# The tokens' half-precision copies: contiguous reads and strided writes in place of strided reads and contiguous writes

## The chip, the cores and the metric

The kernel runs on one core of a Trainium2 chip. The metric is the device time of one execution in microseconds (us); lower is better. The time of a version is the median of its runs. A core has a matrix engine (PE, with its weight loads listed apart as PEld), a vector engine (DVE), an activation engine (ACT), a general engine (POOL), and a queue engine (SP) that here issues nearly all large transfers.

## What is computed

One layer of a streaming encoder over 512 tokens of width 1024. A token mixer (gated spatial mixing beside differential attention) is followed by a layer norm, and then by a mixture of experts: 32 experts in 4 groups, two experts for each token.

```python
def _hier_moe(x, w_group, b_group, w_expert, b_expert, w_gate, w_up, w_down):
    t = x.reshape(B * S, D)
    ...
    def expert_block(args):
        tok, wgt, e = args
        xb = t[tok]
        hb = jax.nn.silu(xb @ w_gate[e]) * (xb @ w_up[e])
        return (hb @ w_down[e]) * wgt[:, None].astype(xb.dtype)
```

In `reference` the result of the mixer goes through `h = _layer_norm(ALPHA * h + mix, ...)`, then `ffn = _hier_moe(h, ...)`, and `_layer_norm(ALPHA * h + ffn, ...)` is the output.

## The kernel before, in words

The first 470 us are the mixer and the router. After the first layer norm the tokens lie in four tiles `h[t]`, each 128 tokens by 1024 channels in single precision; the router has counted each token's place within its expert in `RS`.

The experts are worked through in 13 steps that the code calls pairs (`PER` lists how many experts share a step: 2 or 4). For each step p:

- `gate_up(p, xe)` (L1159, matmuls at L1170) multiplies the step's gathered tokens `xe` by the gate and up weights.
- `slot_info` (L1228) reads token number and weight of each place, `glu` (L1250) forms silu times up, `glu_transpose` (L1257) transposes it.
- `down` (L1277) multiplies by the down weights; `combine` (L1285) spreads the results back over the tokens, and they are added into `y[t]`, which is the same memory as `h[t]`.
- In between, `gather_mm` (L1220, matmuls at L1224) gathers the tokens of the next step with a one-hot matrix made by `one_hot` (L1212, DVE at L1216).

`gather_mm` needs half-precision weights. So each `h[t]`, scaled by 1024, is kept as the sum of two half-precision pieces, `hs[t][0]` and `hs[t][1]`. `split_h(t)` (L1198) makes them: ACT rounds `h[t]` to the first piece (L1202), DVE subtracts that from `h[t]` and rounds the rest to the second (L1203). These run once per kernel, for t = 0 to 3: four ACT and four DVE instructions, each over 128 partitions by 1024 elements.

The pieces are stored in another order than `h[t]`. Channel 4m + i of `h[t]` lies at place 256i + m of a piece, so that `part_block` (L1195) can hand a contiguous block of 128 to each weight load.

The order around the split is fixed by the code (`manual_schedule`, L1635 on): the first `one_hot`, then the four `split_h`, then the second `one_hot`, then step 0. The second `one_hot` stands behind the four DVE instructions of the split on DVE's queue, and the gather in step 0 needs both it and the pieces. On PE's queue the gather stands behind `gate_up(0)` and `slot_info(0)`. The pieces' tiles, `HS`, take memory that was used in the stage before, among it by the tile of weights `sF` that `gate_up(0)` reads.

Weights come in 1 MB chunks into a ring of buffers (`AHEAD` = 21 chunks ahead, L668). SP issues the load of a chunk when the matmuls that read the buffer's former chunk are done, so PE's progress sets when transfers start. After step 0's gather DVE's queue holds the sorting of the experts (L1373 to L1385), eight instructions of `scale_h` (L1209, L1210) and the second part of the first down result (L1282).

Of the kernel before, what the change touches and what calls it, by code (L numbers as in the profile page):

```python
# [48 lines left out]
def hybrid_block(ctx: ExitStack, tc: tile.TileContext, x, w_in, b_in, sg_ln_g, sg_ln_b, sg_w, sg_b,  # L49
# [35 lines left out]
    def mkpool(stack, name, side):  # L85
        return stack.enter_context(tc.tile_pool(name=name, bufs=1, side=side, reuse_waits="tile"))
# [553 lines left out]
    hp = mkpool(ctx, "hp", "left")  # L640
    h = [hp.tile([128, D], F32, name=f"h{t}") for t in range(NT)]
# [449 lines left out]
    with tc.manual_schedule():  # L1091
# [51 lines left out]
        t = NT - 1  # L1143
# [44 lines left out]
    hs = {}  # L1188
# [8 lines left out]

    def split_h(t):  # L1198
        hs[t] = [HS[t // 2][:, 2 * (t % 2) + j] for j in range(2)]
        hp = h[t].rearrange("q (m i) -> q i m", i=4)  # L1200
        ha, hb = [v.rearrange("q (i m) -> q i m", i=4) for v in hs[t]]
        S.activation(ha, hp, AF.Copy, scale=HSCALE)  # L1202
        V.scalar_tensor_tensor(hb, hp, HSCALE, ha, op0=OP.mult, op1=OP.subtract)  # L1203

# [430 lines left out]
    with tc.manual_schedule():  # L1635
        load_chunks(0, AHEAD + 7)
        ohf = one_hot(0)
        for t in range(NT):
            split_h(t)
        nxt = one_hot(1)  # L1640
        tok1 = mv.tile([128, T], F32, name="tok1", tag="tok1")
        G.iota(tok1, pattern=[[1, T]], base=1, channel_multiplier=0, allow_small_or_imprecise_dtypes=True)
        for p in range(OVERFLOW_AFTER + 1):
            gu, ohf, nxt, xe = pair(p, gu, ohf, nxt)
# [36 lines left out]
```

## Time and profile before

| what | value |
|---|---|
| median of 3 runs | 952.56 us |
| lowest and highest run | 948.33 and 954.31 us |
| the profiled execution's own time | 953.16 us |
| its span, from first to last instruction | 951.6 us |
| PE busy | 901.0 us (95%) |
| DVE busy | 428.1 us (45%) |
| ACT busy | 292.8 us (31%) |
| PE's mean granted clock, share of full speed | 0.982 |

The profiled execution takes 1.56 us more than its span, for what lies around it, and is 0.60 us above the median. Busy shares are means over stages with different limits, so a row is read in the stretch in which it stands. In the rows below, a line as L1202 is the line of the kernel, `out<-in` are the program's tiles, and `128x1024` is partitions by elements.

### The profile page before, as it was taken

How to read it: one execution, taken by the hardware profiler on the slowest of the kernel's cores; microseconds unless marked ns; L12 is line 12 of the kernel's file. 1: busy time of each engine (PE TensorE's matmuls, PEld its weight loads, DVE VectorE, ACT ScalarE, POOL GpSimd, SP SyncE). 2: the span in 40 equal slices, each digit the busy share in tenths (PEclk: the TensorE clock that was granted, in tenths of full speed). 3: DMA queues.
4: the chain of work that ended last, by engine and by line, in shares of the span. 5: the costliest groups of instructions: out<-in, count | busy, mean ns of one | idle time of the engine just before them, and what ended most of it. 6: DMA issues, size and time to landing. Idle time of an engine off the chain costs nothing.

```text
span 951.6 us, 13677 instructions
## 1 busy us (share of the span) xinstructions
PE 901.0 (95%) x5231; PEld 583.1 (61%) x5232; DVE 428.1 (45%) x904; ACT 292.8 (31%) x527; POOL 58.0 (6%) x114
## 2 busy tenths in 40 slices
PE   8999999999999999999989999776779999999997
PEld 6989898986888888888844444222224444444434
DVE  3557676767953333244776332203013342233236
ACT  3356475667841332232441110101001111011213
POOL 5010101011010100020000000000000000000002
PEclk9999999999999999999999999998889999999999
DMA  8535343533143377865587999999999999999972
GB/s 223 144 108 154 91 137 96 137 105 104 63 118 89 121 277 253 295 247 200 192 322 291 417 419 419 419 419 419 418 418 419 420 417 421 418 420 419 389 236 89
DMA packets 80598, 256.11 MB, mean 269 GB/s; under 512 B 9112, under 2 KB 30672, under 8 KB 59536
## 3 DMA queue, kind: packets, MB, share of 16 engines
q1 hardware_dynamic: 79216, 252.36, 70.4%
q0 software_dynamic: 1312, 2.83, 1.4%
q8 instruction: 43, 0.70, 0.3%
q14 instruction: 27, 0.22, 0.1%
HBM read 244.67 MB, written 2.10 MB: 259 GB/s over the span
## 4 chain that ended last, share of the span: by engine, by line
PE 75%; DMA 15%; DVE 7%; ACT 1%; issue 1%; SPq 0%; DVEq 0%; ACTq 0%
PE ps_acc L1170 14%; PE ps_acc L142 7%; PE ps_acc L143 7%; PE ps_acc L144 7%; PE ps_acc L1272 7%; PE ps_w L142 4%; PE ps_w L143 4%; PE ps_w L144 4%; PE ps_w L1289 4%; PE ps_acc L1224 3%; DMA sE<-in_w_down_dram 3%; DMA sO<-in_w_gate_dram 2%; DMA sZ<-in_w_up_dram 2%; DMA sW<-in_w_gate_dram 2%; DMA sS<-in_w_up_dram 2%; DMA sX<-in_w_down_dram 2%
## 5 line engine op out<-in xcount | busy, mean ns | idle before, releaser
L119 DVE TENSOR_TENSOR sW<-wraw,sW 128x1024 fp32r<-128x1024 f32 (+1 forms) x38 | 46.5, 1224 | 98.6 <-ACT sW L118 98.5
L118 ACT CAST sW<-wraw 128x1024 fp32r<-128x1024 f32 (+1 forms) x38 | 39.1, 1030 | 117.5 <-PE ps_w L144 65.8
L142 PE MATMUL ps_acc<-sX,sW 128*128 128x512 f32 x184 | 73.3, 398 | 0.0
L144 PE MATMUL ps_acc<-sX,sW 128*128 128x512 f32 x184 | 72.2, 393 | 0.0
L143 PE MATMUL ps_acc<-sX,sW 128*128 128x512 f32 x184 | 72.0, 391 | 0.0
L1239 DVE TENSOR_REDUCE tid<-ps_w 128x1 f32<-128x2 f32 x11 | 1.7, 159 | 144.4 <-PE ps_w L1234 144.4
L1170 PE MATMUL ps_acc<-sX,xe 128*64 128x512 f32 (+1 forms) x176 | 58.2, 616 | 7.2 <-DMA sX<-in_w_up_dram 7.2
L1282 DVE SCALAR_TENSOR_TENSOR olo<-ps_acc,ws,ohi 128x512 fp32r<-128x512 f32 x22 | 16.5, 750 | 107.8 <-ACT ohi L1281 107.8
L1170 PE MATMUL ps_acc<-sO,xe 128*64 128x512 f32 (+1 forms) x240 | 62.0, 603 | 2.9 <-DMA sO<-in_w_gate_dram 1.5
L1224 PEld LDWEIGHTS <-hs 128*128 128x128 f16 x768 | 45.5, 100 | 21.3 <-issue 21.1
L1292 DVE TENSOR_TENSOR h<-h,ps_w 128x512 f32<-128x512 f32 x88 | 54.4, 679 | 7.9 <-PE ps_w L1289 7.9
L1281 ACT ACTIVATE ohi<-ps_acc,ws 128x512 fp32r<-128x512 f32 x22 | 15.1, 687 | 133.2 <-PE ps_acc L1272 128.3
L1224 PE MATMUL ps_acc<-oh,hs 128*128 128x128 f16 x768 | 52.0, 223 | 2.8 <-DVE oh L1216 2.8
L1170 PE MATMUL ps_acc<-sE,xe 128*64 128x512 f32 (+1 forms) x168 | 50.7, 683 | 1.4 <-DMA sE<-in_w_gate_dram 1.4
L1170 PE MATMUL ps_acc<-sS,xe 128*64 128x512 f32 (+1 forms) x152 | 49.6, 594 | 1.4 <-DMA sS<-in_w_up_dram 1.4
L1170 PE MATMUL ps_acc<-sW,xe 128*64 128x512 f32 (+1 forms) x112 | 45.4, 622 | 5.8 <-DMA sZ<-in_w_up_dram 5.8
L1272 PE MATMUL ps_acc<-sS,hT 128*32 128x512 f32 (+1 forms) x112 | 42.6, 631 | 2.8 <-DMA sS<-in_w_down_dram 2.8
L1170 PE MATMUL ps_acc<-sZ,xe 128*64 128x512 f32 (+1 forms) x120 | 40.3, 609 | 1.5 <-DMA sZ<-in_w_up_dram 1.5
L262 DVE TENSOR_TENSOR sW<-wraw,sW 128x1024 fp32r<-128x1024 f32 x31 | 38.3, 1241 | 6.3 <-ACT sW L258 6.3
L1263 ACT COPY hT<-ps_w 128x512 f32<-128x512 f32 x11 | 6.4, 585 | 112.2 <-PE ps_w L1260 112.2
L1272 PE MATMUL ps_acc<-sW,hT 128*32 128x512 f32 (+1 forms) x80 | 35.1, 646 | 5.1 <-DMA sW<-in_w_down_dram 5.1
L144 PEld LDWEIGHTS ps_acc<-sX,sW 128*128 128x128 f32 x184 | 34.5, 188 | 7.4
(399 smaller groups left out, 2000.0 us busy)
## 6 DMA issues: line engine op xcount, KB each, us to landing
wraw<-in_w_in_dram SPq DMA_DIRECT2D x32, 512.0 KB, 3.7
sX<-in_w_up_dram SPq DMA_DIRECT2D x16, 1024.0 KB, 17.9
sS<-in_w_down_dram SPq DMA_DIRECT2D x14, 1024.0 KB, 17.5
sO<-in_w_up_dram SPq DMA_DIRECT2D x14, 1024.0 KB, 19.8
sO<-in_w_gate_dram SPq DMA_DIRECT2D x13, 1024.0 KB, 19.7
sX<-in_w_down_dram SPq DMA_DIRECT2D x13, 1024.0 KB, 16.0
sS<-in_w_gate_dram SPq DMA_DIRECT2D x12, 1024.0 KB, 16.1
sE<-in_w_gate_dram SPq DMA_DIRECT2D x12, 1024.0 KB, 19.8
```

The source lines that it names most:

```text
L118: S.copy(hi, src)
L119: V.tensor_sub(lo, src, hi.bitcast(F32))
L142: P.matmul(o, lhsT=lh, rhs=rh, start=first, stop=False)
L143: P.matmul(o, lhsT=lh, rhs=rl, start=False, stop=False)
L144: P.matmul(o, lhsT=ll, rhs=rh, start=False, stop=last)
L262: V.tensor_sub(usplit[i][1], uraw[i], usplit[i][0].bitcast(F32))
L1170: P.matmul(o[j * w:(j + 1) * w, :], lhsT=xe[:, k, j * w:(j + 1) * w], rhs=chunk(p, m, j, k), start=k == ks[0], stop=k == ks[-1], skip_grou ...
L1224: P.matmul(pg[d // 4][:, (d % 4) * 128:(d % 4 + 1) * 128], lhsT=part_block(hs[t][j], d), rhs=ohf[:, t], start=d % 4 == 0 and t == 0 and j ...
L1272: P.matmul(po[j * w:(j + 1) * w, :], lhsT=hT[:, k, j * w:(j + 1) * w], rhs=chunk(p, 2 + n, j, k), start=k == 0, stop=k == 3, skip_group_ch ...
L1282: V.scalar_tensor_tensor(ol, po, ws, oh.bitcast(F32), op0=OP.mult, op1=OP.subtract)
L1289: P.matmul(pcs[t], lhsT=ohT[:, t * 128:(t + 1) * 128], rhs=o, start=i == 0, stop=i == 1)
L1292: V.tensor_add(yn, yn, pcs[t])
```

## The change

`split_h` walks both operands in another order. Before, the inner loop of each instruction goes over m: the single-precision input is read with a step of 4 elements (16 bytes) and the half-precision output is written one element after the other. After the change the inner loop goes over i: the input is read in memory order, and each output element lands 256 elements (512 bytes) from the one before it. Every fourth element starts a new run, 2 bytes on. The DVE instruction has the first piece, `ha`, as its second input; it is read in the same order as the output is written, in memory order before and with the step of 512 bytes after.

```diff
     def split_h(t):
         hs[t] = [HS[t // 2][:, 2 * (t % 2) + j] for j in range(2)]
-        hp = h[t].rearrange("q (m i) -> q i m", i=4)
-        ha, hb = [v.rearrange("q (i m) -> q i m", i=4) for v in hs[t]]
+        hp = h[t].rearrange("q (m i) -> q m i", i=4)
+        ha, hb = [v.rearrange("q (i m) -> q m i", i=4) for v in hs[t]]
         S.activation(ha, hp, AF.Copy, scale=HSCALE)
         V.scalar_tensor_tensor(hb, hp, HSCALE, ha, op0=OP.mult, op1=OP.subtract)
```

The values and where they are stored stay the same. Nothing moves: every engine has the same instructions in the same order, and only the access patterns of the four ACT and four DVE instructions differ.

## Rows read from the trace of the kernel before

**Rows 1.** The page, part 1 (busy time and share of the span) and, from part 2, the DMA rate in 40 equal slices of 23.8 us each.

```profile
PE 901.0 (95%) x5231; PEld 583.1 (61%) x5232; DVE 428.1 (45%) x904; ACT 292.8 (31%) x527; POOL 58.0 (6%) x114
...
GB/s 223 144 108 154 91 137 96 137 105 104 63 118 89 121 277 253 295 247 200 192 322 291 417 419 419 419 419 419 418 418 419 420 417 421 418 420 419 389 236 89
```

**Rows 2.** The chain of waits from 440 to 560 us, in order of time: start, length, what.

```profile
471.38 2.75 PE ps_acc L1170 x12
474.14 5.56 DMA sE<-in_w_down_dram
479.70 7.95 DVE hs L1203 x4
487.65 0.61 DVE oh L1216
488.30 1.86 PE ps_acc L1224 x16
```

**Rows 3.** The timeline from 464 to 512 us: start, length, engine, line, operation; in brackets the idle time before it and what ended it.

```profile
474.87 0.20 ACT L1052 ACTIVATE warm<-eps_c 128x1 f32<-128x1 f32 x1
...
476.38 0.69 DVE L1216 TENSOR_TENSOR oh<-io,RW 128x512 f16<-128x512 f32 x1
...
476.51 1.03 PE L1170 MATMUL ps_acc<-sF,xe 128*64 128x512 f32 x4
...
477.58 8.07 ACT L1202 ACTIVATE hs<-h 128x1024 f16<-128x1024 f32 x4 [2.51 <-PE ps_acc L1170]
...
479.69 7.96 DVE L1203 SCALAR_TENSOR_TENSOR hs<-h,hs 128x1024 f16<-128x1024 f32 x4 [2.62 <-DMA sE<-in_w_down_dram]
...
485.38 0.10 PEld L1224 LDWEIGHTS <-hs 128*128 128x128 f16 x1
...
487.56 0.68 DVE L1216 TENSOR_TENSOR oh<-io,RW 128x512 f16<-128x512 f32 x1
...
488.30 1.86 PE L1224 MATMUL ps_acc<-oh,hs 128*128 128x128 f16 x16 [2.75 <-DVE oh L1216]
...
489.96 1.06 PE L1260 MATMUL ps_w<-ident,sl 128*128 128x128 f32 x4
```

**Rows 4.** The two lines of the split, instruction by instruction: shortest, median and longest in ns, first and last start in us.

```profile
L1202 ACT ACTIVATE hs<-h x4: 2075/2093/2115, 477.6 to 483.6; 128x1024 f16<-128x1024 f32 x4
```

```profile
L1203 DVE SCALAR_TENSOR_TENSOR hs<-h,hs x4: 1958/2047/2072, 479.7 to 485.7; 128x1024 f16<-128x1024 f32 x4
```

**Rows 5.** Groups by line with shapes kept apart, over the whole span: busy us and mean ns of one, then idle time before. All but the two last read and write in memory order; those two are the split's.

```profile
L118 ACT CAST sW<-wraw 128x1024 fp32r<-128x1024 f32 x36 | 37.9, 1053 | 116.0 <-PE ps_w L144 65.8 <-PE ps_acc L144 29.1 <-DMA wraw<-in_w_out_dram 11.7
```

```profile
L501 DVE SCALAR_TENSOR_TENSOR hsel<-hw 128x1024 fp32r<-128x1024 f32 x1 | 1.2, 1192 | 0.0
```

```profile
L1202 ACT ACTIVATE hs<-h 128x1024 f16<-128x1024 f32 x4 | 8.1, 2094 | 2.5 <-PE ps_acc L1170 2.5
```

```profile
L1203 DVE SCALAR_TENSOR_TENSOR hs<-h,hs 128x1024 f16<-128x1024 f32 x4 | 8.0, 2031 | 2.6 <-DMA sE<-in_w_down_dram 2.6
```

**Rows 6.** The same groups in the stretch from 470 to 510 us, for one line at two sizes. L1070 writes half-precision elements 6 bytes apart (every third place of a tile).

```profile
L1070 DVE TENSOR_SCALAR W<-RW 128x104 f16<-128x104 f32 x1 | 0.3, 260 | 0.0
...
L1070 DVE TENSOR_SCALAR W<-RW 128x24 f16<-128x24 f32 x1 | 0.2, 186 | 0.0
```

**Rows 7.** Busy time by stretches of 2.5 us: PE, PEld, DVE, ACT and POOL (with counts), then PE's granted clock, the DMA share and GB/s.

```profile
485.00:487.50 2.50, 0.55 (x10) 0.29 (x9) 2.50 (x2) 1.13 (x2) 0.00 (x0) 1.00 0.99 419
487.50:490.00 2.50, 1.70 (x17) 1.70 (x17) 2.12 (x7) 0.00 (x0) 0.00 (x0) 0.61 1.00 423
490.00:492.50 2.50, 2.50 (x27) 2.08 (x26) 0.95 (x9) 1.07 (x2) 0.00 (x0) 0.70 1.02 429
492.50:495.00 2.50, 2.50 (x17) 0.97 (x16) 1.96 (x6) 0.10 (x1) 0.00 (x0) 1.00 0.55 229
```

**Rows 8.** The timeline of PE alone from 515 to 527 us: the same matmuls in the next step of the experts.

```profile
522.55 1.05 PE L1224 MATMUL ps_acc<-oh,hs 128*128 128x128 f16 x16
523.90 0.75 PE L1260 MATMUL ps_w<-ident,sl 128*128 128x128 f32 x4 [0.29 <-DVE sl L1253]
```

**Rows 9.** Busy time by longer stretches, columns as in rows 7.

```profile
495.00:500.00 5.00, 4.44 (x39) 2.73 (x35) 4.86 (x11) 0.69 (x1) 0.00 (x0) 1.00 0.77 257
500.00:505.00 5.00, 4.36 (x19) 1.92 (x21) 3.93 (x11) 0.00 (x0) 0.00 (x0) 1.00 0.54 185
...
510.00:515.00 5.00, 5.00 (x26) 1.64 (x24) 4.89 (x9) 0.00 (x0) 0.00 (x0) 1.00 0.46 169
...
520.00:530.00 10.00, 9.71 (x89) 5.13 (x85) 1.57 (x6) 1.27 (x2) 0.00 (x0) 1.00 1.01 423
...
850.00:900.00 50.00, 49.26 (x320) 22.79 (x318) 15.03 (x33) 9.77 (x21) 1.05 (x2) 1.00 1.00 410
```

**Rows 10.** What SP's queue waited for from 470 to 952 us: us in total, times, longest.

```profile
SPq L719 <- PE ps_acc L1170: 41.0, 22, 12.3
SPq L719 <- PE ps_acc L1272: 37.2, 11, 10.4
```

**Rows 11.** The chain of waits from 488 to 952 us, without PE's pieces: three stretches of it on DVE early, then the first and the last of a run of transfers.

```profile
491.38 0.20 DVE keys L1373
...
499.07 0.67 DVE olo L1282
...
573.24 13.17 DMA sW<-in_w_down_dram
...
687.80 19.76 DMA sE<-in_w_down_dram
```

## The prediction

> **What bounds the kernel now.** I read the page first: PE is busy 95% of the span, DVE 45% and ACT 31% [rows 1]. That would make an edit on ACT and DVE worth nothing, but it is a mean over stages. So I looked next at the chain of waits where the split stands. It goes through DVE: four split instructions for 7.95 us, the second one-hot for 0.61, and only then the gather on PE [rows 2]. This is the one place where the edit can touch the end.
>
> The timeline shows the mechanism [rows 3]. ACT is free at 475.07 and starts its first split instruction at 477.58. The last matmuls on the tile sF end at 476.51 + 1.03 = 477.54, and the pieces' tiles take that memory, so this start does not depend on the change. DVE's first split starts at 479.69. The profile names a transfer as its releaser, but the first ACT instruction ends at 477.58 + 2.09 = 479.67 [rows 3, 4], and DVE needs its result; I take ACT as the releaser. DVE then runs to 487.65, the one-hot to about 488.24, and PE starts the gather at 488.30. PE had its first gather weights at 485.38 and stood idle for 2.75 us. So
>
> gather start = 477.58 + a + 4d + 0.65,
>
> with a one ACT instruction and d one DVE instruction (start to start when DVE is the slower). Before: 477.58 + 2.11 + 7.96 + 0.65 = 488.30, which is the row.
>
> Does a shift here reach the end? The DMA rate is 417 to 421 GB/s from the 23rd slice to the 37th, about 523 to 880 us [rows 1], and from 573 to 707 us the chain is a run of transfers [rows 11]. But between 495 and 515 us the DMA share is only 0.77, 0.54 and 0.46 in three stretches of 5 us [rows 9]: the queue waits there for PE to give buffers free, 78.2 us in two kinds of waits from 470 us on [rows 10]. If PE runs x us earlier at 488, the buffers come free x earlier, the transfers reach their full rate x earlier, and the same bytes end x earlier. I take the shift as passed on whole, in both directions. It also goes through DVE's chain of sorting and scaling from 491.38 to 499.07 us [rows 11], which starts from PE's work behind the gather and moves with it.
>
> **The change, part by part.** No instruction is added, removed or moved. Eight instructions get other access patterns, and each has a part that becomes cheaper and a part that may become dearer.
>
> What the step of 16 bytes costs in reading: an ACT copy of 128x1024 in memory order takes 1053 ns, the split's 2094, a difference of 1.04 us. A DVE instruction of the same kind in memory order takes 1192 ns, the split's 2031, a difference of 0.84 us [rows 5]. The output type is no likely cause: the one-hot also writes half precision, and its 128x512 takes 0.68 us, a little over half of 1192 ns [rows 3, 5].
>
> ACT, four instructions. The read becomes contiguous (minus 1.04 us each), the write gets a step of 512 bytes. No row shows such a write. The nearest spaced write is L1070, with 6 bytes between elements: 260 ns for 104 elements and 186 for 24, so (260 - 186) / 80 = 0.93 ns an element, against 1192 / 1024 = 1.16 ns in memory order with the fixed part included [rows 5, 6]. The spacing there costs nothing. The other nearest row is the split's own strided read, (2094 - 1053) / 1024 = 1.02 ns more an element. So a lies between 1.05 us and 2.09 us. I take 1.05: the L1070 row is at least a write. It is a weak choice, since 6 bytes are far from 512, and I keep both ends.
>
> DVE, four instructions. The read of h becomes contiguous, but the read of the first piece gets the step of 512 bytes, and the write too. One strided stream is exchanged for two. The strided read has a price in the rows, 0.84 us, and I take it for the piece as well. So d stays at 2.03 us if two strided streams run beside each other as one does, and that is what I take. Below, d = 1.19 if a step of 512 bytes is free everywhere. Above, the prices add: 1.19 + 2 x 0.84 = 2.87.
>
> The sum: with a = 1.05 and d unchanged, the gather starts at 477.58 + 1.05 + 7.96 + 0.65 = 487.24, that is 1.06 us earlier. PE still idles for about 1.7 us, so DVE still sets the start. Of ACT's saving of 4 x 1.04 = 4.2 us, only the first instruction's lies on the path; the other three run beside DVE's first three, which are longer. If that cover were gone (d under a), ACT's four would set the start instead.
>
> PE's granted clock is 0.61 in the stretch from 487.5 to 490 us and 0.70 from 490 to 492.5, behind the idle time; before and after it is 1.00 [rows 7]. Sixteen gather matmuls take 1.86 us there and 1.05 in the next step; four transposes take 1.06 and 0.75 [rows 3, 8]. So the lower clock costs about 0.81 + 0.31 = 1.1 us. With 1.7 us of idle time left I count none of it back; all of it is the bound, and the range keeps it.
>
> [...] The rows show that a step of 16 bytes in reading nearly doubles an instruction [rows 5]. [...]
>
> **The rivals.**
> Nothing changes in the sum: a strided write costs ACT what the strided read did, a = 2.09, and d = 2.03. For it speaks that the priced step is the only one that the rows show at 16 bytes or more; against it L1070. It gives 953.16, and 952.6 as a median. [...]
>
> Everything becomes cheap: a = 1.05, d = 1.19. DVE ends at 477.58 + 1.05 + 4.76 = 483.4, the one-hot at about 484.1, before PE asks at 485.38. The gather then starts 2.9 us earlier, and with the clock kept up to 1.1 more: 949.2 to 950.3 in the profiled execution's terms, about 949 as a median. Against it: the piece is read with a step that no row shows as free.
>
> Slower, by DVE's two strided streams. With a = 2.09 and d = 2.87 the gather starts at 477.58 + 2.09 + 11.48 + 0.65 = 491.8, 3.5 us later: 956.1 as a median. It decides from d = 2.25 on if ACT gets cheap (1.05 + 4d over 10.07), and from d = 2.0 if it does not. If each scattered write of 2 bytes costs twice a strided read, a = 1.05 + 2.08 = 3.13 and d = 1.19 + 0.84 + 1.68 = 3.71; the gather starts 7.9 us later, 960.5. A loss of over 1% (9.5 us) needs dearer writes still, d of about 4.1 with a of 3.3. For it speaks that the edit gives DVE one strided stream more; against it that no row shows any such stall on a write.
>
> **How the numbers follow.** The profiled execution took 953.16 us; 953.16 - 1.06 = 952.1. It stands 0.60 above the median of the three runs, so the median should go to 951.5. Chances: this forecast 0.33, no change in the sum 0.27, everything cheap 0.12, two streams that add 0.18, dearer writes 0.10. The runs before lie from 948.33 to 954.31 us, so a median of runs can be off by 2 or so from scatter alone. The range from 947 to 957 holds the first four cases with that scatter and leaves out the dear writes and the edges, about 2 in 10. A measurement of this kernel can tell about 1%, 9.5 us, from no change. No gain here can come to that, since the stall is 2.75 us and the clock's part 1.1; I leave 0.01 for scatter. Over 1% slower has 0.04, from the dear end of the writes; within 1% is 0.95.
>
> **What would show it.** In the changed kernel: L1202 at about 1.05 us each, if the write is free, or near 2.1. L1203 near 2.0, or 1.2, or 2.9. The first DVE split should start about 1.05 us after the first ACT one; PE's wait before L1224 for the one-hot should fall from 2.75 to about 1.7 us, and the chain of waits still pass L1203. The first expert load behind 490 us should be issued as much earlier as the gather starts. The prediction is wrong if L1203 gets longer than 2.25 us, if it falls under L1202, or if the gather's shift does not come back at the end.

## The result and the profile after

The changed kernel takes 965.09 us as the median of 4 runs (963.82 to 966.50), the kernel before, with a fourth run, 952.48 us. The ratio is 1.0141, with a 95% interval of 1.0121 to 1.0161: 12.6 us, 1.4% slower. The forecast was 951.5 us, in a range from 947 to 957.

The profiled execution has a span of 963.2 us. The two lines of the split come first: shortest, median and longest in ns, first and last start in us.

```profile
L1202 ACT ACTIVATE hs<-h x4: 4781/5063/5096, 474.5 to 487.9; 128x1024 f16<-128x1024 f32 x4
```

```profile
L1203 DVE SCALAR_TENSOR_TENSOR hs<-h,hs x4: 4706/4708/4712, 479.3 to 493.0; 128x1024 f16<-128x1024 f32 x4
```

Against [rows 4] both take 2.3 to 2.4 times as long. ACT's 2.09 us have become 4.78 (for the first; the next ones' 5.06 overlap a little, and the four take 18.52 us together), DVE's 2.05 have become 4.71.

The chain of waits from 470 to 520 us, in order of time (start, length, what):

```profile
474.48 4.79 ACT hs L1202
...
479.29 18.45 DVE hs L1203 x4
497.74 0.53 DVE oh L1216
...
498.31 1.86 PE ps_acc L1224 x16
...
501.36 0.19 DVE keys L1373
```

It is the chain of [rows 2] with the same links. In the prediction's formula, with ACT's start of this execution: 474.48 + 4.79 + 18.45 + 0.65 = 498.37; the row has 498.31. From ACT's start to the gather it takes 23.83 us, against 10.72 before [rows 3]: 13.1 us more. What PE waited for from 470 us to the end (us in total, times, longest), the longest first:

```profile
PE ps_acc L1224 <- DVE oh L1216: 15.9, 1, 15.9
```

The wait of 2.75 us [rows 3] has become 15.9. Behind it the transfers run dry, as the busy time in stretches of 5 us shows (PE, PEld, DVE, ACT, POOL, PE's granted clock, DMA share, GB/s):

```profile
485.00:490.00 5.00, 0.00 (x0) 0.00 (x0) 5.00 (x2) 5.00 (x2) 0.00 (x0) 0.75 1.01 424
490.00:495.00 5.00, 0.00 (x0) 0.00 (x0) 5.00 (x2) 3.43 (x2) 0.00 (x0) 0.50 0.04 18
495.00:500.00 5.00, 1.69 (x17) 1.69 (x17) 4.62 (x7) 0.00 (x0) 0.00 (x0) 0.50 0.00 0
500.00:505.00 5.00, 5.00 (x42) 3.10 (x42) 2.93 (x15) 1.17 (x2) 0.00 (x0) 0.88 0.01 2
```

PE does nothing for 15.9 us, so no buffer comes free, and from 490 to 505 us the DMA share is 0.04 or less, where it was 0.46 or more in the rows shown of before [rows 7, 9]. SP's first load after 490 us is issued about 6.4 us behind the gather's start in both kernels. First before, then after:

```profile
494.78 0.33 SPq L719 DMA_DIRECT2D sO<-in_w_up_dram  x1
```

```profile
504.69 0.33 SPq L719 DMA_DIRECT2D sO<-in_w_up_dram  x1
```

While PE is idle its granted clock falls: 1.00 from 482.5 to 485 us, 0.75 from 485 to 490 and 0.50 from 490 to 500 us.

How 13.1 us become 11.6 in the span: this execution reached the split 3.1 us earlier, as the stages before it scatter (ACT's start is at 474.48, not 477.58, and lies from 474.76 to 477.57 in the five variants below). The sorting on DVE starts at 501.36 instead of 491.38 [rows 11], which is 13.1 - 3.1 = 10.0 us later, and it stays near that to the end stage. The last 1.6 us arise at the end. There 12 matmuls that only keep PE busy take longer in this execution; PE's granted clock is 0.83 from 945 to 955 us, where before it was 1.00 from 935 to 945. First before, then after:

```profile
L1622 PE MATMUL ps_acc<-ones_b,zero_b x12: 379/379/389, 938.1 to 942.2; 128*128 128x512 bf16 x12
```

```profile
L1622 PE MATMUL ps_acc<-ones_b,zero_b x12: 379/488/631, 948.0 to 953.8; 128*128 128x512 bf16 x12
```

No experiment was made on this. In the profiles of all five variants below, three of which also start the gather late, the same matmuls have a median of 379 ns as before. So it is not something that a late gather always brings.

### The profile page after: what moved, and what is told of

Same layout as the page of the kernel before. It is cut to its first block, busy times and chain, and to the rows that moved or that the text cites. A ratio compares the mean times of both kernels' runs of the same rounds, so it can differ in the third digit from the quotient of the medians.

```text
span 963.2 us, 13677 instructions
## 1 busy us (share of the span) xinstructions
PE 903.4 (94%) x5231; PEld 582.0 (60%) x5232; DVE 438.9 (46%) x904; ACT 303.6 (32%) x527; POOL 58.0 (6%) x114
## 4 chain that ended last, share of the span: by engine, by line
PE 76%; DMA 12%; DVE 8%; ACT 2%; issue 1%; SPq 0%; DVEq 0%; ACTq 0%
PE ps_acc L1170 15%; PE ps_acc L1272 7%; PE ps_acc L142 7%; PE ps_acc L143 7%; PE ps_acc L144 7%; PE ps_w L142 4%; PE ps_w L144 4%; PE ps_w L143 4%; PE ps_w L1289 4%; PE ps_acc L1224 3%; DMA sW<-in_w_gate_dram 2%; DMA sZ<-in_w_up_dram 2%; DMA sO<-in_w_up_dram 2%; DMA sE<-in_w_down_dram 2%; DVE hs L1203 2%; DMA sS<-in_w_up_dram 2%
## 5 line engine op out<-in xcount | busy, mean ns | idle before, releaser
L1170 PE MATMUL ps_acc<-sX,xe 128*64 128x512 f32 (+1 forms) x176 | 61.0, 660 | 6.0 <-DMA sX<-in_w_up_dram 6.0
L1224 PE MATMUL ps_acc<-oh,hs 128*128 128x128 f16 x768 | 51.6, 222 | 15.9 <-DVE oh L1216 15.9
L1170 PE MATMUL ps_acc<-sS,xe 128*64 128x512 f32 (+1 forms) x152 | 51.9, 611 | 1.0 <-DMA sS<-in_w_up_dram 1.0
L1252 ACT ACTIVATE sl<-ps_acc 128x512 f32<-128x512 f32 x13 | 8.1, 621 | 97.5 <-PE ps_acc L1170 97.5
```

What stands on the lines that cost most here:

```text
L1170: P.matmul(o[j * w:(j + 1) * w, :], lhsT=xe[:, k, j * w:(j + 1) * w], rhs=chunk(p, m, j, k), start=k == ks[0], stop=k == ks[-1], skip_grou ...
L1224: P.matmul(pg[d // 4][:, (d % 4) * 128:(d % 4 + 1) * 128], lhsT=part_block(hs[t][j], d), rhs=ohf[:, t], start=d % 4 == 0 and t == 0 and j ...
```

## The experiments

Each version was timed beside new runs of the kernel before, whose median was 952.54 us for one group of versions and 950.85 for the other; losses and gains below go by the ratio to it. Line numbers move by a line or two between versions.

The question was what in the new order makes one instruction take 4.7 us: the write as such, the step of 512 bytes, the innermost loop of 4 elements, writes that cover only half of a 4-byte word, DVE's second strided stream, or the two engines disturbing each other.

**The steps one by one.** A kernel that does nothing of the layer runs instructions of the split's size, three times each, and varies one operand. The core of it:

```python
S.activation(wide[:, 0:8192:8], h[0], AF.Copy, scale=HSCALE)   # writes 16 bytes apart
...
V.scalar_tensor_tensor(wide[:, 0:8192:8], h[0], HSCALE, a, op0=OP.mult, op1=OP.subtract)
```

> This kernel leaves out the whole layer: it copies x to the output after a list of ACT copies and DVE scalar_tensor_tensor instructions of 128x1024, each three times, that differ only in the step of one operand; the engines run one after the other, and at the end both do the changed split at once. Theory A, the write alone: a half-precision element written away from the last one costs about 4.4 ns on either engine, so every write step from some small size on gives about 4.7 us (16, 32, 64 and 512 bytes alike, inner loop of 64 or of 4 alike), and DVE's strided second input costs no more beside it. Theory B, the step of 512 bytes: writes at 16 to 64 bytes, or at 520, take about 2.1 us (the price of the strided read) and only 512 gives 4.7. Theory C, the inner loop of 4: the 512-byte step with an inner loop of 64 takes about 1.1 to 2.1 us, and the strided second input with an inner loop of 4 also takes over 4 us though its write is contiguous. Theory D, partial words: single-precision writes at 16 or 64 bytes take about 2.1 us where half-precision ones take 4.7, and runs of 2 or more neighbours cost less per element in proportion.

The groups of ACT with shapes kept apart (busy us, mean ns of one, idle before). The lines in order: half-precision writes in memory order (L68), 4 (L70), 8 (L72), 16 (L74) and 64 bytes apart (L78), 512 apart with an innermost loop of 64 (L80) and of 4, as in the change (L82), 520 apart (L84), runs of two neighbours 64 bytes apart (L86); single-precision writes 16 bytes apart (L94) and 1024 apart with an innermost loop of 4 (L98); the old split's read with a step of 16 bytes (L100); half-precision reads 512 bytes apart (L104).

```profile
L74 ACT ACTIVATE wide<-h 128x1024 f16<-128x1024 f32 x3 | 14.4, 4788 | 0.1
L80 ACT ACTIVATE wide<-h 128x1024 f16<-128x1024 f32 x3 | 14.3, 4753 | 0.1
L82 ACT ACTIVATE wide<-h 128x1024 f16<-128x1024 f32 x3 | 14.2, 4748 | 0.1
L84 ACT ACTIVATE wide<-h 128x1024 f16<-128x1024 f32 x3 | 14.2, 4731 | 0.1
L78 ACT ACTIVATE wide<-h 128x1024 f16<-128x1024 f32 x3 | 13.9, 4644 | 0.1
...
L72 ACT ACTIVATE wide<-h 128x1024 f16<-128x1024 f32 x3 | 7.5, 2513 | 0.1
L100 ACT ACTIVATE wide<-h 128x1024 f16<-128x1024 f32 x3 | 6.0, 2000 | 0.1
L94 ACT ACTIVATE wide<-h 128x1024 f32<-128x1024 f32 x3 | 6.0, 1998 | 0.1
L98 ACT ACTIVATE wide<-h 128x1024 f32<-128x1024 f32 x3 | 5.9, 1952 | 0.1
...
L104 ACT ACTIVATE wide<-a 128x1024 f16<-128x1024 f16 x3 | 5.8, 1922 | 0.1
...
L70 ACT ACTIVATE wide<-h 128x1024 f16<-128x1024 f32 x3 | 4.0, 1344 | 0.1
L86 ACT ACTIVATE wide<-h 128x1024 f16<-128x1024 f32 x3 | 3.2, 1063 | 0.1
L68 ACT ACTIVATE wide<-h 128x1024 f16<-128x1024 f32 x3 | 3.2, 1057 | 0.1
```

Theory B falls: 16 bytes cost as much as 512, and 520 as much. Theory C falls: the innermost loop of 64 is no faster than that of 4. Theory A holds from 16 bytes on (32 bytes apart, L76, it takes 4.48 us, the least of these rows), but not below, where the time about halves with the step (2.51 us at 8 bytes, 1.34 at 4). Theory D stands: a 4-byte write with a step of 16 bytes or more takes 1.92 to 2.0 us, about what a strided read takes, and only the 2-byte write takes 4.5 to 4.8; two neighbours at a time take 1.06 us, as writes in memory order do.

DVE alone, all with the output in half precision: writes 512 bytes apart (L123), the second input read 512 bytes apart with the write contiguous (L145), both as in the change (L147), all contiguous (L109).

```profile
L123 DVE SCALAR_TENSOR_TENSOR wide<-h,a 128x1024 f16<-128x1024 f32 x3 | 14.1, 4706 | 0.1
L147 DVE SCALAR_TENSOR_TENSOR wide<-h,a 128x1024 f16<-128x1024 f32 x3 | 14.1, 4705 | 0.1
...
L145 DVE SCALAR_TENSOR_TENSOR wide<-h,a 128x1024 f16<-128x1024 f32 x3 | 5.7, 1895 | 0.1
...
L109 DVE SCALAR_TENSOR_TENSOR wide<-h,a 128x1024 f16<-128x1024 f32 x3 | 3.7, 1224 | 128.8 <-ACT wide L107 128.7
```

DVE has the same price, and the strided second input costs 0.67 us by itself and nothing beside the write: these two streams don't add. (No row has both inputs strided with the write contiguous, so whether two strided reads add is not shown. The test of both engines at once came out otherwise than meant: DVE's four instructions were scheduled early, beside ACT's writes at 8 and 16 bytes, and took 4.73 to 4.96 us there. The next two experiments answer that.)

**One engine at a time.** First only ACT walks the new order, then only DVE.

```diff
-        S.activation(ha, hp, AF.Copy, scale=HSCALE)
+        hn = h[t].rearrange("q (m i) -> q m i", i=4)
+        na, nb = [v.rearrange("q (i m) -> q m i", i=4) for v in hs[t]]
+        S.activation(na, hn, AF.Copy, scale=HSCALE)
```

> Only ACT's instruction is walked in the new order; DVE's keeps the strided read and the contiguous write. If the write's price is each engine's own: ACT at 4.8 us alone and 4.5 to 4.6 from start to start, DVE at 2.03 and waiting for ACT, gather start about 4.8 + 3 x 4.55 + 2.03 + 0.65 = 21.1 us after ACT's start against 10.7 before, so about 10.4 us slower, nearly as much as the whole change (13.1 us in the profile). If ACT is slow only because DVE writes beside it, ACT falls to under 4 us and the loss to under 7 us.

963.36 us against 952.54 of the kernel before, ratio 1.0112 (1.0070 to 1.0154), 10.7 us slower. The timeline from 470 to 520 us (start, length, engine, line, operation):

```profile
476.48 18.47 ACT L1204 ACTIVATE hs<-h 128x1024 f16<-128x1024 f32 x4 [2.50 <-PE ps_acc L1170]
...
494.98 1.96 DVE L1205 SCALAR_TENSOR_TENSOR hs<-h,hs 128x1024 f16<-128x1024 f32 x1 [2.55 <-ACT hs L1204]
...
497.59 1.86 PE L1226 MATMUL ps_acc<-oh,hs 128*128 128x128 f16 x16 [13.15 <-DVE oh L1218]
```

Then DVE alone, with the same `hn`, `na` and `nb` as above:

```diff
...
-        V.scalar_tensor_tensor(hb, hp, HSCALE, ha, op0=OP.mult, op1=OP.subtract)
+        V.scalar_tensor_tensor(nb, hn, HSCALE, na, op0=OP.mult, op1=OP.subtract)
```

> Only DVE's instruction is walked in the new order; ACT's keeps the strided read and the contiguous write. If the write's price is each engine's own: ACT at 2.09 us, DVE at 4.7 and 4.6 from start to start, gather start about 2.1 + 18.4 + 0.65 = 21.1 us after ACT's start, about 10.4 us slower than before; the whole change is 2.7 us slower still by ACT's first instruction. If the two engines slow each other, DVE falls to under 4 us and the loss to under 8 us.

962.91 us, ratio 1.0117 (1.0071 to 1.0164), 11.1 us slower. The same view:

```profile
475.04 8.18 ACT L1204 ACTIVATE hs<-h 128x1024 f16<-128x1024 f32 x4 [2.51 <-PE ps_acc L1170]
477.15 18.44 DVE L1205 SCALAR_TENSOR_TENSOR hs<-h,hs 128x1024 f16<-128x1024 f32 x4 [2.62 <-ACT hs L1204]
...
496.15 1.87 PE L1226 MATMUL ps_acc<-oh,hs 128*128 128x128 f16 x16 [13.15 <-DVE oh L1218]
```

The gather starts 21.1 us after ACT's start in both, as expected. ACT is as slow without DVE's scattered writes, and DVE without ACT's. The price is each engine's own, and the two prices don't add in time since the engines work side by side.

**Words or neighbours.** A second list of instructions, with runs that start in the middle of a 4-byte word.

> This kernel too leaves out the whole layer: x plus a row of instructions of 128x1024, three times each, ACT first and then DVE. Theory D2, from the first list: a visit to 16 bytes costs about 1.8 ns when whole 4-byte words are read or written, and about 4.5 ns when a written word is only half covered, whatever the step; an instruction takes the longer of that and its contiguous time. Then: half-precision writes 6 bytes apart visit 384 stretches of 16 bytes and take about 1.9 us, 4 bytes apart 1.34, 8 bytes apart 2.5; aligned pairs of neighbours 64 bytes apart 1.06; the same pairs moved by one element (two half words each, 512 visits) 2.5 us; groups of four moved by one 1.34; groups of eight moved by one (two visits each) 1.3; single-precision writes 8 bytes apart 1.1 and 16 apart 2.0; reads at 8 bytes 1.1, at 16 bytes 2.0, of either type. Rival: a run of two neighbours is what counts, not the 4-byte word. Then the moved pairs take 1.06 us like the aligned ones.

ACT's groups: writes 8 bytes apart (L77), pairs 64 bytes apart moved by one element (L81) and aligned (L79), writes 6 bytes apart (L73), groups of eight moved by one (L85), writes 4 bytes apart (L75), groups of four moved by one (L83).

```profile
L77 ACT ACTIVATE wide<-h 128x1024 f16<-128x1024 f32 x3 | 7.4, 2472 | 0.1
L81 ACT ACTIVATE wide<-h 128x1024 f16<-128x1024 f32 x3 | 7.3, 2436 | 0.1
...
L73 ACT ACTIVATE wide<-h 128x1024 f16<-128x1024 f32 x3 | 5.7, 1909 | 0.1
L85 ACT ACTIVATE wide<-h 128x1024 f16<-128x1024 f32 x3 | 4.7, 1553 | 0.0
L75 ACT ACTIVATE wide<-h 128x1024 f16<-128x1024 f32 x3 | 4.0, 1337 | 0.1
L83 ACT ACTIVATE wide<-h 128x1024 f16<-128x1024 f32 x3 | 4.0, 1317 | 0.1
...
L79 ACT ACTIVATE wide<-h 128x1024 f16<-128x1024 f32 x3 | 3.2, 1066 | 0.1
```

On DVE the same writes cost much the same: 2.46 us at 8 bytes (L109), 2.42 for the moved pairs (L113), 1.34 at 4 bytes (L107). Its writes 6 bytes apart and in memory order are needed below:

```profile
L105 DVE SCALAR_TENSOR_TENSOR wide<-h,b 128x1024 f16<-128x1024 f32 x3 | 5.6, 1872 | 0.1
...
L103 DVE SCALAR_TENSOR_TENSOR wide<-h,b 128x1024 f16<-128x1024 f32 x3 | 3.7, 1226 | 47.6 <-ACT wide L89 47.5
```

The moved pairs take 2.44 us where the aligned ones take 1.07: it is the half-covered word, and the rival falls. All but one row come as the theory has them; the groups of eight moved by one take 1.55 us, not 1.3; why is left open. Reads and 4-byte writes on ACT take 1.09 to 1.12 us at 8 bytes and 1.99 to 2.04 at 16, as expected. The price per visit follows from three rows: 256 visits to a stretch of 16 bytes take 1.34 us (L75), 512 take 2.47 (L77), 1024 take 4.79 (L74 of the first list), so the added visits cost 1.13 us / 256 = 4.4 ns and 2.32 us / 512 = 4.5 ns each.

**Pairs in the kernel.** ACT alone writes two neighbours, then jumps 512 bytes; DVE is left as before.

```diff
-        S.activation(ha, hp, AF.Copy, scale=HSCALE)
+        S.activation(hs[t][0].rearrange("q (i m a) -> q m i a", i=4, a=2),
+                     h[t].rearrange("q (m a i) -> q m i a", i=4, a=2), AF.Copy, scale=HSCALE)
```

> Only ACT's instruction differs from the kernel before: it writes two neighbours (4 bytes), then jumps 512 bytes, and reads h with steps of 16 bytes. DVE keeps its old order. If half-covered words are the price, ACT takes about 2.0 us, as before, and the time stays at about 952.5 us, against the 963.4 of the run in which ACT wrote one element at a time. If the 512-byte jump itself were the price, ACT would take about 2.4 us or more (half the jumps) and the split would end 1 to 2 us later; if the innermost loop's shortness were, still longer.

950.14 us against 950.85, ratio 0.9991 (0.9971 to 1.0011): no change that can be told, and by the two ratios 1.2% less than where ACT alone wrote single elements. ACT's line:

```profile
L1202 ACT ACTIVATE hs<-h x4: 1283/1290/1298, 474.8 to 478.3; 128x1024 f16<-128x1024 f32 x4
```

The gather in its timeline:

```profile
484.65 1.05 PE L1225 MATMUL ps_acc<-oh,hs 128*128 128x128 f16 x16 [1.92 <-DVE oh L1217]
```

The 512-byte jump does not bring 4.8 us when whole words are written: ACT takes 1.29. That it would take 2.0 us was wrong; 1.29 is less than with the old read (2.09). The read here goes back and forth between two neighbouring stretches of 16 bytes; why that is cheaper than a step to a new one each time is left open. The run also comes near the case that the prediction forecast, ACT cheaper and DVE as before: the gather starts 9.89 us after ACT's start (474.76), 0.83 less than before. PE's wait falls from 2.75 to 1.92 us, its granted clock is 1.00 from 485 to 490 us, and the 16 matmuls take 1.05 us instead of 1.86.

**One tile of the four.**

```diff
+        walk = "q m i" if t == 3 else "q i m"
-        hp = h[t].rearrange("q (m i) -> q i m", i=4)
-        ha, hb = [v.rearrange("q (i m) -> q i m", i=4) for v in hs[t]]
+        hp = h[t].rearrange("q (m i) -> " + walk, i=4)
+        ha, hb = [v.rearrange("q (i m) -> " + walk, i=4) for v in hs[t]]
```

> Only the last of the four tiles (t = 3) is split in the new order. By the formula of the gather's start with the measured durations: ACT 3 x 2.0 + 4.8 = 10.8 us after its start, DVE 4.7 more, one-hot 0.65: 16.2 us against 10.7 before, so 5.4 us slower, about 958 us. If the loss came from something else than the sum along this chain (the transfers behind it, the clock after the idle time), it would be about a quarter of the whole change, 3 us, or nearly all of it.

957.92 us against 950.85, ratio 1.0067 (1.0044 to 1.0089), 4.2 to 8.5 us slower. In its timeline ACT's four start at 477.57 and the gather starts at 493.62:

```profile
493.62 1.87 PE L1225 MATMUL ps_acc<-oh,hs 128*128 128x128 f16 x16 [8.08 <-DVE oh L1217]
```

That is 16.05 us after ACT's start, where the formula gave 16.2, and 5.3 us more than before. The loss is the sum along the chain, not a share of something behind it: a quarter of the whole change, 3 us, lies outside the interval.

**The step given to the weight loads.** The split reads and writes in memory order, and the gather's weight loads take every fourth element.

```diff
-        return v[:, d % 4 * 256 + d // 4 * 128:d % 4 * 256 + d // 4 * 128 + 128]
+        return v[:, d // 4 * 512 + d % 4:d // 4 * 512 + 512:4]
...
+        ha, hb = hs[t]
+        S.activation(ha, h[t], AF.Copy, scale=HSCALE)
+        V.scalar_tensor_tensor(hb, h[t], HSCALE, ha, op0=OP.mult, op1=OP.subtract)
```

> The split reads and writes in memory order, and the gather's weight loads read the pieces with a step of 4 elements (8 bytes) instead. Split: ACT 1.05 us, DVE 1.19 us each, done before PE asks, so the gather starts 2.9 us earlier and 3 to 4 us come back. If the step is free for weight loads the kernel takes about 949 us; if a strided weight load costs half as much again (100 to 150 ns, 50 ns more for each of 768 loads) it takes about 949 + 38 = 987 us.

949.51 us against 952.54, ratio 0.9971 (0.9954 to 0.9989): 3.0 us faster than the kernel before by the medians, and by the ratio the fastest of all versions (the one with pairs has 0.9991). The timeline from 470 to 506 us:

```profile
476.84 3.90 ACT L1201 ACTIVATE hs<-h 128x1024 f16<-128x1024 f32 x4 [2.50 <-PE ps_acc L1170]
...
477.94 4.63 DVE L1202 SCALAR_TENSOR_TENSOR hs<-h,hs 128x1024 f16<-128x1024 f32 x4 [1.60 <-ACT hs L1201]
...
484.67 1.06 PE L1223 MATMUL ps_acc<-oh,hs 128*128 128x128 f16 x16
```

The wait is gone: DVE and its one-hot are done before PE asks, the gather starts 7.83 us after ACT's start (10.72 before), and its 16 matmuls take 1.06 us. That is less than the 1.86 of before because the clock no longer falls (1.00 from 482.5 to 490 us); at the full clock they took 1.05 before as well [rows 8]. A weight load itself takes 115 ns in the mean of its 768, where it took 100 before. So a step of 8 bytes costs the weight loads 15 ns each, of which the matmuls show next to nothing.

## Why the prediction was wrong

**The place and the chain: right.** The gather's start is 477.58 + a + 4d + 0.65 in form, with ACT's first instruction and DVE's four on the path. Counted from each execution's own ACT start and with the measured a and d, it gives the start to 0.1 us or so, in the changed kernel and with DVE alone. Where ACT is the slower (ACT alone, one tile), its four and DVE's last set the start, as the prediction had it for d under a, and that fits as closely.

**The shift passed on whole: right.** 13.1 us at the gather against 12.6 at the end by the medians, 10.4 against 10.7 and 11.1 with one engine, and 5.3 against 6.4 with one tile. In the version with the step at the weight loads the gather starts 2.9 us earlier and its matmuls, at the full clock, save about 0.8 more, against 3.0 at the end. Each of these shifts lies within the interval of its ratio. SP's next load was issued as much later as the gather started.

**The clock's part: too low, without weight here.** The prediction left about 1.7 us of idle time and in its sum counted none of the lower clock's cost back, though its range kept it. In the profile of the run with pairs PE still waits 1.92 us, but its clock stays at 1.00 and the gather's 16 matmuls save their 0.8 us.

**The price of the write: wrong, and this decided.** The step that failed is "So a lies between 1.05 us and 2.09 us", and with it the bound 2.87 for d. The upper end was the price of a strided read, taken over to a write. It holds for 4-byte writes (1.92 to 2.0 us), but these are 2-byte writes, and a half-covered word costs 4.4 to 4.5 ns a visit: a = 4.79, d = 4.6 from start to start. The price asked was no longer bounded by any row, and I should have kept the upper end open.

**The row I leaned on: misleading.** L1070 has 6-byte steps on DVE, and at 0.93 ns an element I read it as free. Over 1024 elements the same step takes 1.87 us on DVE (L105 of the second list) against 1.23 in memory order (L103), and 1.91 on ACT (L73) against 1.06. Why L1070's two sizes, 24 and 104 elements, did not show it is not tested and stays open.

**DVE's two strided streams: no part of it.** The second input's step costs 0.67 us alone and nothing beside the write. My rival on the other side had the right sign by the wrong mechanism; the case of dearer writes (0.10) had the right one, sized at a = 3.13 and d = 3.71 and so at 960.5 us. I had put only 0.04 on over 1%, for d of about 4.1 and more; it measured 4.6.

**No change in the sum: wrong for this write.** The rival had a strided write pay what the strided read paid, which would have left the time unchanged. The 4-byte writes do so (1.92 to 2.0 us, the strided read 2.0), the 2-byte writes do not (4.7 us).

## What to carry to other kernels

Where a layout has to be permuted, put the strided side where the rows show that it is cheap: here the weight loads took it for next to nothing (115 ns each in the mean instead of 100, the gather's 16 matmuls 1.06 us against 1.05 at the full clock before), while on ACT strided reads took 1.9 times as long as reads in memory order (2.00 us against 1.06) and scattered 2-byte writes 4.5 times (4.75 us; on DVE 1.6 and 3.8 times, 2.00 and 4.71 us against 1.22). If half-precision data must be scattered by ACT or DVE, write aligned pairs of neighbours, so that whole 4-byte words are covered (1.06 to 1.29 us on ACT and 1.23 to 1.26 on DVE, where single elements 16 bytes or more apart took 4.4 to 4.8). And when no row of the trace shows an operation, the nearest row of another kind is no upper bound for it.

## What was unexpected of the hardware

A half-precision write that covers half of a 4-byte word costs 4.4 to 4.5 ns for each stretch of 16 bytes that is visited, on ACT and on DVE alike: 1024 of them take 4.4 to 4.8 us, whether the next one is 16, 32, 64 or 512 bytes away; as many elements 8 bytes apart, with half the stretches, take 2.4 to 2.5 us, and 4 bytes apart 1.3. On ACT the same 1024 elements as aligned pairs 64 bytes apart take 1.06 us, as fast as contiguous ones; moved by one element, 2.44 us.
